# A two-layer hybrid decoder: inputs laid out as blocks, and the first stage's modulation wholly on TensorE in four column blocks beside ten feature tiles of w_in

## The chip, the core and the metric

The kernel runs on one core of a Trainium2 chip. The metric is the device time in microseconds of one execution, the median of several runs. Beside it stands one profiled execution, whose span, from its first to its last instruction, all rows of the trace are measured in. PE is TensorE (matmuls), DVE VectorE, ACT ScalarE, POOL GpSimd; SP issues most of the DMAs.

## What is computed

256 tokens of 2048 features go through two layers, each with a token-mixing block and a gated MLP of 5632 features, both behind a modulated RMS norm whose shift, scale and gate come from a conditioning vector c:

```python
cond = jax.nn.silu(c)
for l in range(DEPTH):
    mods = cond @ w_ada[l] + b_ada[l]
    sh1, sc1, g1, sh2, sc2, g2 = [m[:, None, :] for m in jnp.split(mods, 6, axis=-1)]
    h = rms_norm(x, norm_pre_mix[l]) * (1.0 + sc1) + sh1
    y = token_mixing(h, ...)           # proj = h @ w_in[l]; four head groups; concat @ w_out[l]
    x = x + g1 * rms_norm(y, norm_post_mix[l])
    h = rms_norm(x, norm_pre_ffn[l]) * (1.0 + sc2) + sh2
    y = conv_ffn(h, ffn_w_in[l], ffn_conv_w[l], ffn_w_out[l])
    x = x + g2 * rms_norm(y, norm_post_ffn[l])
```

w_ada is [2048, 12288] for each layer. The four head groups of token_mixing are a latent attention (MLA), a diagonal state-space model (S5), a sparse attention (NSA) and a gated delta rule (GDN, four heads, a chain of chunk products). All of it is f32.

## The kernel before

**Weights.** A weight tile is 128 x 1024 f32, 512 KB. wload issues its DMA on SP into one of four raw buffers; wsplit makes a high part wh on ACT (line 366) and a low part wl on DVE (line 367), three buffers each; mm3 multiplies the three products of the parts that matter on PE (line 127), 24 matmuls of 256 columns for a feature-major tile. mm3's other operand is the normed input ht, split the same way, or the other way round.

**Modulation.** w_ada passes as tiles of the same size. Most of it is background: ada streams blocks through two rawa buffers and sums 16 tiles on DVE (line 412), a given number of tiles with each weight tile. Only shift and scale of the first norm of layer 0 are needed at once. ada_quarter computes them in four quarters of the features, 16 tiles each, loaded at line 457 in two pieces of 2 KB a partition. Six tiles of a quarter (ADA_DVE) are summed on DVE into acc, ten go to PE as two matmuls with one stationary column, condc, into rows 0 and 32 of a PSUM bank, and acc follows with a column of ones. Quarters 1 to 3 take their tiles from the two rawa and the two rawm buffers in turn. A quarter ends in a copy, four transposes (lines 465 to 478) and the sums that make mod.

**The first stage (run).** x is loaded, its squares summed on ACT (new_squares), its row factors put on a diagonal (set_diag), and pre_norm multiplies x by that diagonal on PE, a quarter of the features at a time, with mod applied on ACT at line 549. Behind each quarter come the w_in tiles that need it: FIRST names three column groups of 256, so 12 tiles in all, the first four loaded ahead. Two of the three feed S5, the third the queries of GDN heads 0 and 1. Meanwhile DVE and ACT build the S5 tables. Some 25 small per-feature vectors are loaded by DMAs of their own and transposed on PE (vectors_ada, vectors); those of layer 1, and the loads of its S5 parameters b and c, stand in the FFN of layer 0.

**The mixers** of a layer follow in this order: S5, the narrow token-major columns (gemm_a), GDN heads 0 and 1 (gdn_half), heads 2 and 3, MLA, NSA, GDN's output gate, then project_out with w_out. The code says what depends on what; a scheduler lays the instructions of each engine in a fixed order, with the priorities that high_priority and the lanes give. So w_in products stand wherever a chain of small steps waits.

## Time and profile before

| what | us |
|---|---|
| median of 3 runs | 2695.22 |
| the three runs | 2687.34 to 2700.55 |
| span of the profiled execution | 2692.3 |
| PE busy in it | 2553.3 (95%) |
| DVE busy | 1924.8 (71%) |
| ACT busy | 1260.7 (47%) |
| end of the first stage (S5's first products) | 162.61 |
| first products of w_out, layer 0 | 527.37 |

For the profiled execution the record has the span; the median of the runs stands 2.9 us above it. The busy time of an engine is summed over its instructions without overlaps. The PE clock of a stretch is the mean of what was granted, 1.0 for 2.4 GHz and 0.5 for 1.2 GHz. The table of stretches gives the busy time of each engine and the mean share of the 16 DMA engines; the timeline joins instructions of one kind that follow each other, and a start is exact while a matmul's end is modelled.

### The profile page before, as it was taken

How to read it: one execution, taken by the hardware profiler on the slowest of the kernel's cores; microseconds unless marked ns; L12 is line 12 of the kernel's file. 1: busy time of each engine (PE TensorE's matmuls, PEld its weight loads, DVE VectorE, ACT ScalarE, POOL GpSimd, SP SyncE). 2: the span in 40 equal slices, each digit the busy share in tenths (PEclk: the TensorE clock that was granted, in tenths of full speed). 3: DMA queues.
4: the chain of work that ended last, by engine and by line, in shares of the span. 5: the costliest groups of instructions: out<-in, count | busy, mean ns of one | idle time of the engine just before them, and what ended most of it. 6: DMA issues, size and time to landing. Idle time of an engine off the chain costs nothing. (4 is left out here: it accounts for less than half of the span.)

```text
span 2692.3 us, 44696 instructions
## 1 busy us (share of the span) xinstructions
PE 2553.3 (95%) x17587; PEld 2257.8 (84%) x17587; DVE 1924.8 (71%) x3036; ACT 1260.7 (47%) x2025; POOL 9.6 (0%) x21
## 2 busy tenths in 40 slices
PE   5899999798999999999998999999899999999998
PEld 2478788687999999988877879888799999998886
DVE  6668888778877777776878888865677655555555
ACT  4244554546545444444545445555544444444443
POOL 0000000000000000000000000000000000000000
PEclk7889999899999999999999999999999999999999
DMA  8986887676888888877776667835588766665554
GB/s 269 298 242 188 259 277 226 202 268 217 274 287 277 283 286 284 293 247 234 232 255 228 189 201 243 267 123 170 180 272 280 224 187 188 183 186 188 188 188 148
DMA packets 325899, 621.43 MB, mean 231 GB/s; under 512 B 45132, under 2 KB 131640, under 8 KB 324152
## 3 DMA queue, kind: packets, MB, share of 16 engines
q1 hardware_dynamic: 317632, 617.36, 71.5%
q8 instruction: 138, 2.26, 0.3%
q10 hardware_dynamic: 8056, 1.21, 0.3%
q14 instruction: 73, 0.60, 0.1%
HBM read 614.26 MB, written 4.23 MB: 230 GB/s over the span
## 5 line engine op out<-in xcount | busy, mean ns | idle before, releaser
L127 PE MATMUL mm<-ht,wh 128*128 128x256 f32 x7232 | 1311.4, 283 | 2.9 <-ACT wh L366 2.9
L366 ACT CAST wh<-raw 128x1024 fp32r<-128x1024 f32 (+1 forms) x740 | 771.2, 1043 | 953.8 <-PE mm L127 751.2
L367 DVE TENSOR_TENSOR wl<-raw,wh 128x1024 fp32r<-128x1024 f32 (+1 forms) x740 | 893.2, 1213 | 346.1 <-ACT wh L366 344.2
L127 PEld LDWEIGHTS mm<-ht,wh 128*128 128x128 f32 x7232 | 1114.1, 189 | 15.2 <-issue 6.8
L127 PE MATMUL mm<-ht,wl 128*128 128x256 f32 x3616 | 1023.9, 283 | 7.9 <-DVE wl L367 7.6
L127 PEld LDWEIGHTS mm<-ht,wl 128*128 128x128 f32 x3616 | 681.7, 189 | 20.2 <-DVE wl L367 12.8
L412 DVE SCALAR_TENSOR_TENSOR acc<-rawa,condc,acc 128x1024 f32<-128x1024 f32 x310 | 397.3, 1282 | 216.5 <-DMA rawa<-in_w_ada_dram 215.0
L127 PE MATMUL mm<-wh,ht 128*128 128x512 f32 (+1 forms) x1600 | 507.4, 395 | 3.4 <-ACT ht L366 2.9
L127 PEld LDWEIGHTS mm<-wh,ht 128*128 128x128 f32 x1600 | 300.9, 189 | 68.0 <-ACT ht L366 3.2
L127 PE MATMUL mm<-wl,ht 128*128 128x512 f32 (+1 forms) x800 | 316.1, 395 | 1.7 <-DVE wl L367 1.7
L127 PE MATMUL mx<-wh,ht 128*128 128x512 f32 x704 | 221.4, 395 | 0.0
L127 PE MATMUL mx<-arena 128*128 128x128 f32 (+8 forms) x1432 | 199.1, 280 | 12.5 <-ACT arena L1417 4.7
L127 PEld LDWEIGHTS mx<-arena 128*128 128x128 f32 (+5 forms) x1432 | 156.0, 170 | 51.4 <-issue 20.2
L127 PEld LDWEIGHTS mm<-wl,ht 128*128 128x128 f32 x800 | 151.6, 190 | 34.0 <-DVE wl L367 3.0
L127 PEld LDWEIGHTS mx<-wh,ht 128*128 128x128 f32 x704 | 132.0, 187 | 32.1
L127 PE MATMUL mx<-wl,ht 128*128 128x512 f32 x352 | 139.3, 396 | 0.9 <-DVE wl L367 0.8
L131 PE MATMUL mx<-ident,arena 128*128 128x128 f32 (+3 forms) x367 | 68.4, 290 | 32.4 <-ACT arena L1280 11.0
L367 DVE TENSOR_TENSOR ht<-arena,ht 128x1024 fp32r<-128x1024 f32 x52 | 63.6, 1223 | 39.4 <-ACT ht L366 39.0
L131 PEld LDWEIGHTS mx<-ident,arena 128*128 128x128 f32 (+3 forms) x367 | 44.4, 148 | 53.7 <-ACT arena L1280 12.7
L1557 DVE SCALAR_TENSOR_TENSOR arena<-mm,v,arena 128x255 f32<-128x255 f32 (+1 forms) x176 | 78.2, 476 | 4.3 <-ACT arena L1555 3.5
L127 PEld LDWEIGHTS mx<-wl,ht 128*128 128x128 f32 x352 | 66.0, 187 | 18.1 <-DVE wl L367 2.1
L366 ACT CAST ht<-arena 128x1024 fp32r<-128x1024 f32 x52 | 54.2, 1050 | 56.5 <-PE mm L127 32.3
(308 smaller groups left out, 1514.1 us busy)
## 6 DMA issues: line engine op xcount, KB each, us to landing
raw<-in_ffn_w_in_dram SPq DMA_DIRECT2D x352, 512.0 KB
rawa<-in_w_ada_dram SPq DMA_DIRECT2D x348, 512.0 KB
raw<-in_ffn_w_out_dram SPq DMA_DIRECT2D x176, 512.0 KB
raw<-in_w_in_dram SPq DMA_DIRECT2D x116, 512.0 KB
raw<-in_w_out_dram SPq DMA_DIRECT2D x64, 512.0 KB
rawm<-in_w_ada_dram SPq DMA_DIRECT2D x28, 512.0 KB
raw<-in_w_in_dram SPq DMA_DIRECT2D x16, 426.0 KB
raw<-in_w_in_dram SPq DMA_DIRECT2D x16, 354.0 KB
```

The source lines that it names most:

```text
L127: self.nc.tensor.matmul(out, lhsT=lhsT, rhs=rhs, start=start, stop=stop)
L131: self.nc.tensor.transpose(out, in_, self.ident[:k, :k])
L366: self.nc.scalar.copy(hi.bitcast(F32R), src)
L367: self.nc.vector.tensor_sub(lo.bitcast(F32R), src, hi)
L412: self.last_mac = self.nc.vector.scalar_tensor_tensor(acc, w, self.condc[:, kc:kc + 1], acc, op0=ALU.mult, op1=ALU.add)
L1557: nc.vector.scalar_tensor_tensor(c[:, s:], ps[m][:, :256 - s], self.fconv(l, 2 - s, f), c[:, s:], op0=ALU.mult, op1=ALU.add)
```

## The change

A function layout on the host writes every weight matrix as a sequence of blocks (class Blocks), one for each tile in the form in which the kernel loads it, so that a tile is one DMA in which each partition's row is contiguous, 4 KB for most. The per-feature vectors become one array vec of 486 columns for each layer, loaded by two DMAs at the start; S5's b and c, the positions, the conditioning vector and a transposed x (xT) are laid out too. The kernel then takes its tiles from blk.

ada_quarter becomes a generator. All 16 tiles go to PE: the stationary operand condz holds a column of c and 31 zeros, and even and odd tiles go to different halves of the bank, so that the two matmuls of two tiles have four column blocks (o = 0, 32, 64, 96). The tiles take turns in two rawa, two rawm and two acc buffers. Four matmuls with ident2 sum the blocks into columns. row_scale takes the squares of xT on ACT, sums them on PE and scales xT on DVE; norm_quarter applies mod on DVE. With that new_squares of layer 0 moves into project_out.

FIRST has five column groups, so 20 w_in tiles of layer 0 stand in the first stage, interleaved with pairs of modulation tiles (the ten feature tiles of 128 columns are those five groups of 256); the keys and values of GDN heads 0 and 1 come with them and their convolutions are early. Layer 1 still takes three of the groups. The S5 tables are built between the tiles of quarters 2 and 3.

The core of the diff (the layout's calls in the rest of the kernel are all of the form of the one in gemms_b):

```diff
-FIRST = (O_U, O_U + 256, O_GQ)      # columns of the first products
...
+FIRST = (O_U, O_U + 256, O_GQ, O_GK, O_GV)
...
+    def blk(self, nm, l, k0, kn, *segs):
+        o, w = BLOCKS[nm].at[k0, kn, segs]
+        src = self.I[nm]
+        return bass.AP(tensor=src.tensor, offset=src.offset + l * BLOCKS[nm].n + o, ap=[[w, P], [1, w]])
...
-    def ada_quarter(self, q, rings, on_dve):
-        """Shift and scale of a quarter of the features for the first block, without delay; on_dve: the chunks whose products
-        go to the vector engine, the others to the tensor engine."""
+    def ada_quarter(self, q):
         nc = self.nc
         bank = self.mx()
-        rows = [bank[32 * i:32 * i + 1] for i in range(2)]
-        src = self.I["w_ada"][0][:, 0:2 * D].rearrange("k (i c) -> k i c", i=2)[:, :, q * 512:(q + 1) * 512]
-        acc = self.acct()
-        for c in range(4):
-            self.mm(bank[0:64, c * P:(c + 1) * P], self.zerob[:, 0:64], self.identb, c == 0, c == 3)
-        def add(col, t, first, last):
+        for kc in range(KT):
+            pool, nm = ((self.rawa, "rawa"), (self.rawm, "rawm"), (self.accp, "acc"))[kc % 3]
+            w = pool.tile([P, 1024], F32, name=nm, tag=nm)
+            nc.sync.dma_start(w, self.blk("w_ada", 0, kc, 1, (q * 512, 512), (D + q * 512, 512)))
             for i in range(2):
-                self.mm(rows[i], col, t[:, i * 512:(i + 1) * 512], first, last)
-        pe = [kc for kc in range(KT) if kc not in on_dve]
-        for kc in range(KT):
-            pool, nm = ((self.raw, "raw"), (self.rawa, "rawa"), (self.rawm, "rawm"))[rings[kc % len(rings)]]
-            w = pool.tile([P, 1024], F32, name=nm, tag=nm)
-            nc.sync.dma_start(w.rearrange("p (i c) -> p i c", i=2), src[kc * P:(kc + 1) * P])
-            if kc in on_dve:
-                self.ada_mac(acc, w, kc, kc == on_dve[0])
-            else:
-                add(self.condc[:, kc:kc + 1], w, kc == pe[0], False)
-        add(self.ones[:, 0:1], acc, False, True)
+                o = 64 * (kc % 2) + 32 * i
+                self.mm(bank[o:o + 32], self.condz[:, kc], w[:, i * 512:(i + 1) * 512], kc < 2, kc >= KT - 2)
+            if kc % 2 and kc < KT - 1:
+                yield
         with self.first():
-            r = self.reg(AT[7], 512)(512)[0:64]
-            nc.scalar.copy(r[:, 0:256], bank[0:64, 0:256])
-            nc.vector.tensor_copy(r[:, 256:512], bank[0:64, 256:512])
+            r = self.small.tile([P, 512], F32, name="hf", tag="hf")
+            nc.scalar.copy(r[:, 0:256], bank[:, 0:256])
+            nc.vector.tensor_copy(r[:, 256:512], bank[:, 256:512])
+            cols = self.mx(8)
             for c in range(4):
-                self.tp(bank[:, c * 64:(c + 1) * 64], r[:, c * P:(c + 1) * P])
-            cols = bank[:, 0:256].rearrange("p (c i z) -> p i c z", i=2, z=32)
+                self.mm(cols[:, 2 * c:2 * c + 2], r[:, c * P:(c + 1) * P], self.ident2[:, 0:64:32], True, True)
+            cols = cols.rearrange("p (c i) -> p i c", i=2)
             for i in range(2):
-                self.ada_out(0, 2 * i + q // 2, cols[:, i, :, 0], 4 * (q % 2))
+                self.ada_out(0, 2 * i + q // 2, cols[:, i], 4 * (q % 2))
...
+    def row_scale(self):
+        nc = self.nc
+        xT = self.ar[:, A_X:A_X + 4096]
+        for i in range(4):
+            nc.sync.dma_start(xT[:, i * 1024:(i + 1) * 1024], self.I["xT"][:, i * 1024:(i + 1) * 1024])
+        r = self.reg(AT[7], 2048)
+        sq, (v, y, a) = (r(512), r(512)), (r(256) for _ in range(3))
+        ss = self.mx(256)
+        for i in range(8):
+            nc.scalar.activation(sq[i % 2], xT[:, i * 512:(i + 1) * 512], AF.Square)
+            for j in range(2):
+                self.mm(ss, self.ones, sq[i % 2][:, j * 256:(j + 1) * 256], i + j == 0, i + j == 8)
+        nc.vector.tensor_scalar(v, ss, 1.0 / D, EPS, op0=ALU.mult, op1=ALU.add)
+        self.rsqrt(v, y, a)
+        for i in range(4):
+            t = xT[:, i * 1024:(i + 1) * 1024].rearrange("p (k t) -> p k t", k=4)
+            nc.vector.tensor_tensor(t, t, y[:, None, :].to_broadcast([P, 4, 256]), op=ALU.mult)
+        self.xr = xT
+    def norm_quarter(self, q):
+        nc = self.nc
+        for k2 in (2 * q, 2 * q + 1):
+            h = self.small.tile([P, 512], F32, name="hf", tag="hf")
+            o = k2 % 2 * 512
+            hi, lo = (self.ht[4 * i + k2 // 2][:, o:o + 512] for i in range(2))
+            for i in range(2):
+                k = 2 * k2 + i
+                sh, sc = (self.mod[:, 0, 2 * j + k // 8, k % 8:k % 8 + 1] for j in range(2))
+                nc.vector.tensor_scalar(h[:, i * 256:(i + 1) * 256], self.xr[:, k * 256:(k + 1) * 256], sc, sh,
+                                        op0=ALU.mult, op1=ALU.add)
+            self.split(h, hi, lo)
...
-    def gemms_b(self, W, cols, nm, kc, pre=()):
-        """Several of them, as a generator that stops after every kc chunks of the contraction; pre: weight tiles loaded
-        ahead."""
+    def gemms_b(self, l, cols, nm, kc, tiles=False):
         kn = 1024 // (nm * P)
-        banks = [self.mmt() for _ in cols]
-        parts = [[b[:, m * 256:(m + 1) * 256] for m in range(nm)] for b in banks]
-        pre = list(pre)
+        parts = [[b[:, m * 256:(m + 1) * 256] for m in range(nm)] for _, b in cols]
         for kk in range(0, KT, kc):
-            for c0, ps in zip(cols, parts):
+            for (c0, _), ps in zip(cols, parts):
                 for k0 in range(kk, kk + kc, kn):
-                    w = self.wsplit(pre.pop(0)) if pre else self.wtile(1024, self.parts_b(W, c0, nm, k0))
+                    w = self.wtile(self.blk("w_in", l, k0, kn, (c0, nm * P)))
                     for ki in range(kn):
                         k = k0 + ki
                         for m in range(nm):
                             o = (ki * nm + m) * P
                             self.mm3(ps[m], [i[:, o:o + P] for i in w], self.hk(k), k == 0 and m == 0,
                                      k == KT - 1 and m == nm - 1)
-            yield
+                    if tiles:
+                        yield
+            if not tiles:
+                yield
...
-    def first_gemms(self, l, pre=()):
-        return self.gemms_b(self.I["w_in"][l], FIRST, 2, KT // 4, pre)
+    def first_gemms(self, l):
+        if l:
+            return self.gemms_b(l, [(c, self.mmt()) for c in FIRST[:3]], 2, KT // 4)
+        self.lane = 0
+        return self.gemms_b(l, [(c, self.mmt() if i < 4 else self.mx()) for i, c in enumerate(FIRST)], 2, KT // 4, True)
...
+        early = [conv(0, i, ps) for i, ps in enumerate(first_qkv)] if l == 0 else []
...
         for tt in range(2):
             self.nc.sync.dma_start(self.x[:, tt], src[tt * P:(tt + 1) * P])
+        if l == 0:
+            self.new_squares()
...
             if not last and g == 0:
                 self.new_squares()
-                rg = self.reg(A_SCR, 800)
-                self.vectors_ada(l + 1, rg)
-                self.vectors(l + 1, rg)
...
         next(constants)
-        self.condition()
         next(constants)
-        rg = self.reg(A_GA + 2560 + P + KT, 800)
-        self.vectors_ada(0, rg)
+        self.vectors()
+        self.lane = 1
+        a = self.ada_quarter(0)
+        next(a)
         self.finish(constants)
+        self.lane = 0
+        self.row_scale()
         self.lane = 1
-        self.ada_quarter(0, (0, 1, 0, 2), ADA_DVE)
-        for tt in range(2):
-            nc.sync.dma_start(self.x[:, tt], xin[tt * P:(tt + 1) * P])
-        self.xx = self.const.tile([P, 8], F32, name="xx")
-        self.new_squares()
-        self.set_diag(self.x_stats())
-        h = self.pre_norm(0, 0)
-        next(h)
-        self.lane = 0
-        self.vectors(0, rg)
-        pre = [self.wload(self.parts_b(self.I["w_in"][0], c0, 2, 0)) for c0 in FIRST[:4]]
-        g = self.first_gemms(0, pre)
-        macs = [self.last_mac]
+        self.finish(a)
+        self.norm_quarter(0)
+        tables = itertools.chain(self.s5_tables(0, nc.scalar, self.ar[:, AT[6]:AT[6] + 1024]),
+                                 self.s5_rotations(0, (self.ar[:, AT[4]:AT[4] + 1024], self.ar[:, AT[5]:AT[5] + 1024])))
+        g = self.first_gemms(0)
         for q in range(1, 4):
             self.lane = 1
-            self.ada_quarter(q, (1, 2), ADA_DVE)
-            macs.append(self.last_mac)
-            self.lane = 0
-            next(g)
-            self.lane = 1
-            if q < 3:
-                next(h)
+            a = self.ada_quarter(q)
+            n = len(FIRST)
+            for i in range(n):
+                next(g)
+                for _ in range(8 * (i + 1) // n - 8 * i // n):
+                    next(a, None)
+                if q > 1:
+                    self.lane = 0
+                    next(tables, None)
+                    next(tables, None)
+                    self.lane = 1
+            self.norm_quarter(q)
         self.lane = 0
-        self.finish(self.s5_tables(0, nc.scalar, self.ar[:, AT[6]:AT[6] + 1024]))
-        with self.after(macs[1]):
-            self.finish(self.s5_rotations(0, (self.ar[:, AT[4]:AT[4] + 1024], self.ar[:, AT[5]:AT[5] + 1024])))
```

**SP at the end of the first stage.** The rows are DMAs in the order of the queue; rawa, rawm and acc hold w_ada, raw holds w_in. Before:

```order
L457 DMA rawa_758<-in_w_ada_dram 128x2x512
L457 DMA rawm_762<-in_w_ada_dram 128x2x512
L349 DMA raw_807<-in_w_in_dram 128x4x256
L349 DMA raw_837<-in_w_in_dram 128x4x256
L349 DMA raw_1154<-in_w_in_dram 128x4x256
L349 DMA raw_1184<-in_w_in_dram 128x4x256
L349 DMA raw_1218<-in_w_in_dram 128x4x256
L349 DMA raw_1535<-in_w_in_dram 128x2x426
```

and after the change:

```order
L406 DMA raw_1157<-in_w_in_dram 128x1024
L406 DMA raw_1250<-in_w_in_dram 128x1024
L406 DMA raw_1280<-in_w_in_dram 128x1024
L406 DMA raw_1314<-in_w_in_dram 128x1024
L406 DMA raw_1344<-in_w_in_dram 128x1024
L406 DMA raw_1377<-in_w_in_dram 128x1024
L406 DMA raw_1736<-in_w_in_dram 128x852
L406 DMA raw_1757<-in_w_in_dram 128x852
L499 DMA rawa_1187<-in_w_ada_dram 128x1024
L499 DMA rawm_1191<-in_w_ada_dram 128x1024
L499 DMA acc_1195<-in_w_ada_dram 128x1024
L499 DMA rawa_1199<-in_w_ada_dram 128x1024
```

The last w_ada tile stood ahead of the w_in tiles; now the last four stand behind eight raw loads.

**PE inside a quarter.** mx1 is the bank of the modulation, the second name of a pair is the stationary column, or the normed input for mm. Before, in the first quarter:

```order
L127 MATMUL mx1_161<-rawa_170,condc_107 1x512 x2
L127 MATMUL mx1_161<-rawm_177,condc_107 1x512 x2
L127 MATMUL mx1_161<-rawa_184,condc_107 1x512 x2
L127 MATMUL mx1_161<-rawm_191,condc_107 1x512 x2
L127 MATMUL mx1_161<-raw_195,condc_107 1x512 x2
```

and after the change, in the second quarter:

```order
L228 MATMUL mx1_323<-acc_362,arena_58 32x512
L228 MATMUL mx1_323<-rawa_366,arena_58 32x512 x2
L228 MATMUL mx1_323<-rawm_370,arena_58 32x512 x2
L228 MATMUL mx1_323<-acc_374,arena_58 32x512 x2
L228 MATMUL mm_290<-ht_59,wh_380 128x256 x2
L228 MATMUL mx1_323<-rawa_408,arena_58 32x512 x2
L228 MATMUL mm_290<-ht_59,wl_381 128x256
```

The products now have 32 columns of output and every ring feeds them; the w_in tiles stand between.

**PE in the chain of GDN heads 2 and 3.** mx with arena alone is a product of the chain, mx with ident a transpose, mm a w_in product, rawm a weight of MLA. Before:

```order
L127 MATMUL mx_3279<-arena 128x128 x4
L127 MATMUL mm<-ht,wl 128x256
L127 MATMUL mm<-ht,wh 128x256 x2
L127 MATMUL mm<-ht,wl 128x256
L127 MATMUL mm<-ht,wh 128x256 x2
L127 MATMUL mm<-ht,wl 128x256
L127 MATMUL mm<-ht,wh 128x256
L127 MATMUL mx_3285<-arena 128x128 x4
L127 MATMUL mm<-ht,wh 128x256
L127 MATMUL mm<-ht,wl 128x256
```

and after the change:

```order
L228 MATMUL mx_3183<-arena 128x128 x4
L228 MATMUL mx_3745<-arena,rawm 128x256 x2
L232 MATMUL mx_3189<-ident,arena 128x128 x4
L228 MATMUL mx_3745<-arena,rawm 128x256 x2
L228 MATMUL mx_3195<-arena 128x128 x4
L228 MATMUL mx_3755<-rawm,arena 128x256 x3
L228 MATMUL mx_3205<-arena 128x128 x4
L228 MATMUL mx_3765<-rawm,arena 128x256 x2
L232 MATMUL mx_3211<-ident,arena 128x128 x4
L228 MATMUL mx_3765<-rawm,arena 128x256
```

The w_in products between the chain's steps are gone, and MLA's products stand there.

## Rows read from the trace of the kernel before

**Rows 1.** The page: busy time, share of the span and instructions of each engine
```profile
PE 2553.3 (95%) x17587; PEld 2257.8 (84%) x17587; DVE 1924.8 (71%) x3036; ACT 1260.7 (47%) x2025; POOL 9.6 (0%) x21
```

**Rows 2.** Stretches of the start: busy us and count by engine, PEclk, DMA share, GB/s
```profile
0.00:10.00 10.00, 1.51 (x7) 0.94 (x7) 4.27 (x18) 0.00 (x0) 3.52 (x10) 1.00 0.70 217
...
35.00:40.00 5.00, 4.09 (x18) 0.58 (x14) 4.72 (x19) 3.81 (x11) 0.00 (x0) 0.93 1.02 415
...
58.00:146.00 88.00, 74.17 (x409) 35.68 (x408) 48.41 (x87) 19.64 (x38) 0.14 (x2) 0.87 0.91 299
```

**Rows 3.** Waits of PE in 0:160 and of SP's queue in 60:150: total, times, longest
```profile
PE mx L127 <- DMA rawa<-in_w_ada_dram: 6.2, 4, 3.1
...
SPq L457 <- PE mx L127: 36.9, 25, 3.9
```

**Rows 4.** PE's timeline, first stage and mixers: start, length, what, count, idle before
```profile
66.63 1.03 PE L127 MATMUL mx<-rawm,condc 128*1 128x512 f32 x4
...
67.58 0.39 PE L127 MATMUL mm<-ht,wl 128*128 128x256 f32 x1
...
83.97 1.03 PE L127 MATMUL mx<-acc,ones 128*1 128x512 f32 x4
...
88.88 0.60 PE L127 MATMUL mx<-rawm,condc 128*1 128x512 f32 x2
...
162.61 0.48 PE L127 MATMUL mx<-arena 64*128 64x128 f32 x2
...
326.79 0.28 PE L127 MATMUL mm<-ht,wl 128*128 128x256 f32 x1
...
332.11 0.28 PE L127 MATMUL mm<-ht,wl 128*128 128x256 f32 x1
```

**Rows 5.** Stretches of the mixers, all work, then the weight products (mm) alone
```profile
162.60:334.70 172.10, 165.14 (x1053) 138.53 (x1053) 146.85 (x296) 81.29 (x156) 0.00 (x0) 0.98 0.75 218
...
334.70:399.40 64.70, 62.48 (x488) 55.47 (x486) 53.73 (x81) 33.22 (x64) 0.52 (x1) 1.00 0.89 278
...
415.20:461.90 46.70, 45.73 (x413) 41.33 (x412) 39.11 (x72) 21.95 (x47) 0.00 (x0) 1.00 0.71 222
...
415.20:461.90 46.70, 26.95 (x157) 20.49 (x156) 1.66 (x4) 1.55 (x4) 1.00 0.71 222
```

**Rows 6.** PE's timeline: first GDN decay, chain products, first products of w_out
```profile
334.69 0.39 PE L127 MATMUL mx<-tri,gg 128*128 128x128 f32 x2
...
461.01 1.08 PE L127 MATMUL mx<-arena 128*128 128x128 f32 x8
...
461.93 0.28 PE L127 MATMUL mx<-ident,ry 128*128 128x128 f32 x1
...
527.37 0.80 PE L127 MATMUL mm<-wh,ht 128*128 128x512 f32 x1 [2.90 <-ACT ht L366]
```

**Rows 7.** DVE's timeline inside the chain of GDN heads 2 and 3
```profile
446.62 1.23 DVE L367 TENSOR_TENSOR wl<-raw,wh 128x1024 fp32r<-128x1024 f32 x1 [0.62 <-ACT wh L366]
...
447.76 0.68 DVE L1030 TENSOR_TENSOR arena<-mx,lmask 128x512 f32<-128x512 f32 x1
```

**Rows 8.** Waits of PE in 770:900 (FFN of layer 0) and 160:480 (mixers)
```profile
PE mx L131 <- DMA rawm<-in_s_c_re_dram: 3.9, 1, 3.9
...
PE mx L131 <- ACT rawm L1280: 1.3, 3, 0.5
...
PE mx L127 <- DMA rawm<-in_nsa_w_v_dram: 2.1, 2, 1.8
...
PE mx L127 <- DMA rawm<-in_mla_w_ukv_dram: 1.2, 1, 1.2
```

**Rows 9.** A stretch of the softmax tail
```profile
505.50:511.00 5.50, 5.50 (x21) 4.20 (x22) 2.73 (x5) 2.88 (x11) 0.00 (x0) 0.58 0.62 179
```

**Rows 10.** ACT's timeline: a square of x, and the last split ahead of w_out
```profile
42.73 0.63 ACT L575 ACTIVATE junk<-arena 128x512 bf16<-128x512 f32 x1
...
526.27 1.04 ACT L366 CAST ht<-arena 128x1024 fp32r<-128x1024 f32 x1 [2.05 <-DVE arena L709]
```

More of the change, by code (lines that the diff above doesn't have):

```diff
@@ L799, in mla @@
                       self.rsin[:, tt, 0:32], 4, 32)
-        wk = part("mla_w_ukv", 2, 0, 4, 256, 0, P)
+        wk = part("mla_w_ukv", 2, range(4), 256, 0, P)
         for hp in range(2):
@@ L807, in mla @@
             nc.scalar.copy(kn[:, 2 * hp:2 * hp + 2], ps.rearrange("p (h t) -> p h t", h=2))
-        wk = part("mla_w_ukv", 2, 0, 4, 256, P, P)
+        wk = part("mla_w_ukv", 2, range(4), 256, P, P)
         for tt in range(2):
@@ L1182, in s5_tables @@
         t = lambda: r(16)
-        are, aim, ls = (self.sld[:, l, i * 16:(i + 1) * 16] for i in range(3))
+        are, aim, ls = (self.vs(l, "s5")[:, i * 16:(i + 1) * 16] for i in range(3))
         step, mag, th, sn, cs, tmp = (t() for _ in range(6))
```

346 lines of the change are left out of this document (171 added, 175 removed).

## The prediction

> **What bounds the kernel now.** The page's first part comes first: TensorE (PE) is busy for 2553.3 us, 95% of the span [rows 1]. A change therefore pays where it takes work off PE, or where it shortens one of the few stretches in which PE is held up. The table by stretches finds the first such stretch at the start. In 58 to 146 us PE has 74.17 busy us of 88 at a mean granted clock of 0.87, while the DMA engines have a share of 0.91 and move 299 GB/s [rows 2]. Two things hold the transfers there. The queue waits of SP show 36.9 us on PE's modulation products: four w_ada buffers are all there is, and PE has to free them. PE in turn waits for w_ada tiles [rows 3]. The PE timeline then gives the milestones [rows 4]: the first stage ends when S5 begins, at 162.61 us, and by then 12 w_in tiles have been multiplied.
>
> The table of the mixers says that from there on PE is the bound for a while: 165.14 busy of 172.10 us before the decay of the first two GDN heads, 62.48 of 64.70 behind it, and 45.73 of 46.70 us during the decay-to-output chain of heads 2 and 3 [rows 5, 6]. Of those 46.70 us, 26.95 hold weight products, which fill the gaps of the chain [rows 5]. Only then comes the attention tail up to the output projection at 527.37 us [rows 6].
>
> **Part 1: eight w_in tiles leave the mixers.** FIRST grows from 3 to 5 column groups, 12 to 20 tiles. In the mixers' pure stretch 45 weight matmuls start between 326.79 and 332.11 us [rows 4], 0.118 us each, so a tile of 24 costs 2.84 us and eight cost 22.7 us. PE is the bound where they stood, so they come off the span there: **-22.7 us**, if the first stage takes them in for nothing.
>
> **Part 2: the end of the first stage.** The order of SP gives what has to come before the last w_ada tile: 64 w_ada tiles, 20 w_in tiles of 0.524 MB, two of 0.436 MB and 2.1 MB of xT, together 47.1 MB. The first 10 us move at a mean of 217 GB/s [rows 2], so about 4 us are lost at the start. The rate is the unknown. From below it is the 299 GB/s of the old stage; from above the 415 GB/s of the five us in which the long rows of x land [rows 2]. The old stage at a full share would be 299/0.91 = 329. I take 355, between the two, as every tile now is one contiguous block and six w_ada buffers stand where four did: 133 us. Behind the last tile come its landing and product, 2 us, the chain from the last product to the next features, 4.9 us (83.97 to 88.88 in the old quarters [rows 4]), and the five w_in tiles that need it, 5 x 2.84 = 14.2 us. In all 4 + 133 + 2 + 4.9 + 14.2 = 158 us against 162.6: **-5 us**. The bounds are 182 (+20) at 299 GB/s and 143 (-20) at 415, rounded.
>
> PE has to keep up with that. Four modulation products of 512 columns take 0.95 us from their start to the next matmul at 66.63 [rows 4], where eight of 128 columns, a quarter of a product each, take 0.92 us [rows 6]: at that rate four in a row would be 1.84 us, so two column groups run side by side. Of such a tile a quarter has 16, so 15 us at two groups and half that at four; five w_in tiles add 14. That is 22 to 29 us of PE for 21 tiles, which need 31 us of transfer at 355 GB/s: close, but covered. DVE loses its six tiles a quarter, which nobody waited for long. The Trainium skill says, in "TensorEngine Tiling (Array Packing)", Tiling Modes, that different tiles of the array can execute in parallel; the trace agrees for two, with the 0.95 us above, and shows none with four. By that rule it is the 22.
>
> One detail is against it. The last four w_ada tiles stand on SP behind eight raw loads, and with four raw and three wh buffers the last of those eight can be issued only when 15 w_in tiles are done on PE. I get that point at about 130 us, in step with the transfers, so I charge nothing; late PE would push it into the end of the stage.
>
> **Part 3: what the mixers lose as cover.** Those tiles were filling. In the new order the chain of GDN heads 2 and 3 has no weight product in it, only about 68 matmul passes of 256 columns of MLA, 8 us at 0.118 us. PE's own work in the old chain is 45.73 - 26.95 = 18.8 us [rows 5]. If the chain keeps its 46.7 us, PE idles for 46.7 - 18.8 - 8 = 20 us; if the weight products were what stretched it, not at all. One look inside decides: at 447.76 DVE begins an eviction that had been standing behind a wl split of 1.23 us that started at 446.62 [rows 7]. About 7.4 tiles stood there by the order of PE, so some 9 us of the chain was such waiting: exposed 11 us, **+11**, with 0 to +20 as bounds.
>
> **Part 4: small loads.** In the FFN of layer 0 PE waits 3.9 us for s5_c_re and 1.3 for the copies behind it, and in the mixers 2.1 us for nsa_w_v and 1.2 us for mla_w_ukv [rows 8]. C of S5 is now one contiguous load without transposes, the layer-1 vectors are two loads at the start, the mixers' tiles are contiguous: up to **-9** with what a clock drop behind the waits costs; at worst 0. I take -8. The row scaling on DVE and ACT, the constants' new place and the S5 tables lie beside the w_ada stream and cost nothing as long as that stream ends the stage; Weights of the rest of the kernel only change layout; PE is the bound there, so nothing.
>
> new_squares of layer 0 now stands in project_out: eight squares of 0.63 us on ACT, seven of them ahead of the last split of the mixers' outputs. ACT was idle for 2.05 us before that split, waiting for DVE, and PE waits 2.90 us for it [rows 6, 10]. So 0 to +4 us; **+1**, because the wait for DVE's norm covers most.
>
> **Sum:** -22.7 - 5 + 11 - 8 + 1 = -23.7 on the profiled span of 2692.3, so 2668.6 us. The median shown, 2695.22, is 2.9 above that span: 2671.5, rounded **2671 us**.
>
> **Rivals.**
> (A) The layout does not do what it says: the queue moves no more than 299 GB/s, or PE frees its buffers no faster. Then the first stage ends at 182 us and -5 becomes +20: 2696 us, no change. For it: the page's DMA share was already 0.91 [rows 2], with pieces of 2 KB. Against: 36.9 us of queue waits on PE at four buffers [rows 3]. The Trainium skill, "DMA: Bandwidth & Descriptors", Specifications, asks for at least 512 B for full rate, and 1 and 2 KB pieces are above that; by that rule the longer rows would bring nothing and the time would be A's. The 415 GB/s of the 8 KB rows of x speak for some gain.
> (B) The mixers are a chain, not PE's work: from the first decay (334.69) to the output projection (527.37) stay 192.7 us [rows 6]. In the new order weight products of 4.3 tiles more, 12 us, stand between the first stage and that decay, so it comes at 158 + 172.1 + 12 = 342 and the projection at 535, 7.5 us later than now. With -8 + 1 behind it and 2.9 to the median: 2696 us, no change.
> (C) Four column blocks at once and 415 GB/s: the stage ends at 143. Then -20 instead of -5: 2656 us.
> (D) The slower side: the uncovered chain drops PE's clock. Around the softmax tail, where PE idles, the granted clock reads 0.58 [rows 9], near the lower level of 1.2 GHz. If heads 2 and 3 run so, their 18.8 us of PE work take twice as long and nothing of B's chain shrinks: 2696 + 18.8 = 2715 us. It decides from the point where the uncovered chain takes longer than the old 46.7 us. Against it: MLA's products and half the evictions are still there, and the chain loses DVE's wl splits.
>
> **How the numbers follow.** Forecast 0.50 (2656 to 2687 by its own bounds on rate and cover), A 0.13, B 0.12, C 0.15, D 0.10. The predicted time is the forecast's, 2671. The range goes from 2646 to 2704: it holds A, B and C's centre and leaves out D and the far half of C's spread. A measurement of this kernel tells 0.5%, 13.5 us, from no change, so faster means under 2681.7. Faster: C and nine tenths of the forecast's half, and a little of A and B, 0.65; same: most of A and B and a little of the forecast, 0.24; slower: D and the tails, 0.11.
>
> **What would show it.** Right: S5's first products at 150 to 165 us with 20 tiles done, over 330 GB/s from 20 to 130 us, modulation products four to a start; the projection at about 505 to 515 us; PE waits of some 10 us inside the second GDN chain; no wait for s5_c. Wrong: a first stage that ends beyond 175 us (A, and the SP row where the last four w_ada tiles wait says whether the raw loads did it); a projection at or after 527 us with idle PE (B), with a granted clock near 0.5 to 0.6 in the second chain (D). A gain outside layer 0's first 530 us and its FFN's S5 loads would be one that I do not see.

## The result and the profile after

The changed kernel takes 2716.6 us (2708.3 to 2720.9) where the kernel before took 2694.0 (2687.3 to 2700.6) on the same chip: 1.0093 times as long, 95% interval 1.0069 to 1.0116. It is slower by 22.6 us; 2671 was predicted, with a range that ended at 2704. The profiled execution of after has a span of 2706.5 us, 14.2 more than before's.

The page's first part, and three rows of the stretches of the first stage (columns as in [rows 2]):

```profile
PE 2579.7 (95%) x17604; PEld 2283.8 (84%) x17604; DVE 1909.8 (71%) x3018; ACT 1258.6 (47%) x2001; POOL 10.2 (0%) x22
...
43.00:73.60 30.60, 25.72 (x147) 14.97 (x146) 22.35 (x41) 5.89 (x8) 0.28 (x2) 0.88 0.70 262
73.60:128.80 55.20, 48.00 (x321) 27.98 (x321) 14.94 (x36) 20.20 (x48) 0.00 (x0) 0.97 0.60 225
...
155.80:174.30 18.50, 7.28 (x27) 1.76 (x26) 4.12 (x11) 2.07 (x4) 0.00 (x0) 0.70 0.88 323
```

Only the first 43 us move more than before (345 GB/s against 289). From there to 128.8 us the queue stays under before's 299 GB/s [rows 2]: the DMA share falls to 0.60 while PE is busy for 48.00 of 55.20 us. The waits of SP's queue and of PE in 0:192 say who held whom (total, times, longest):

```profile
SPq L499 <- PE mx L228: 90.5, 21, 10.9
...
PE mx L228 <- DMA rawa<-in_w_ada_dram: 8.7, 3, 8.2
```

SP waits 90.5 us for PE to free w_ada buffers; of these 61.4 lie in 60 to 150 us, where before it waited 36.9 [rows 3]. PE's timeline shows why, and the milestones (start, length, what, count, idle before):

```profile
23.00 0.60 PE L228 MATMUL mx<-rawm,arena 128*32 128x512 f32 x2
23.02 0.60 PE L228 MATMUL mx<-acc,arena 128*32 128x512 f32 x2
23.43 0.60 PE L228 MATMUL mx<-rawm,arena 128*32 128x512 f32 x2
...
110.18 1.05 PE L228 MATMUL mx<-acc,arena 128*32 128x512 f32 x2
111.16 0.39 PE L228 MATMUL mm<-ht,wl 128*128 128x256 f32 x1
...
164.18 1.92 PE L228 MATMUL mx<-rawa,arena 128*32 128x512 f32 x4 [8.16 <-DMA rawa<-in_w_ada_dram]
...
191.48 1.24 PE L228 MATMUL mx<-arena 64*128 64x128 f32 x8
...
369.04 0.39 PE L228 MATMUL mx<-tri,gg 128*128 128x128 f32 x2
...
530.20 0.50 PE L228 MATMUL mm<-wh,ht 128*128 128x512 f32 x1 [1.59 <-ACT ht L423]
...
581.84 1.22 PE L228 MATMUL mx<-ident,ry 128*128 128x128 f32 x4 [5.14 <-DVE ry L256]
```

An f32 product leaves two records, and the two products of a w_ada tile four. At 23 us four column blocks do run at once: four records start together every 0.43 us. Where one product stands alone between weight products (110.18), its two records follow each other and hold PE for 0.98 us, as much as the four records of a whole tile before [rows 4]. The third quarter takes 42.1 us (83.7 to 125.8), not 31, and PE is busy for most of it:

```profile
83.70:125.80 42.10, 36.84 (x242) 21.39 (x241) 11.39 (x27) 18.28 (x45) 0.00 (x0) 1.00 0.66 250
```

The modulation products hold PE for 15.5 of these 36.84 us, the weight products for 16.2, transposes and table products for 5; PE's waits are 5.1 us, all for ACT and none for a DMA. The last four w_ada tiles, behind eight raw loads on SP, cost an 8.16 us wait. So S5 starts at 191.48, not at 162.61 [rows 4], the first GDN decay at 369.04, not at 334.69 [rows 6].

That decay is 34.4 us late. Not quite half of it comes back behind the decay: NSA's last spread (the row at 581.84) stood at 563.22 before, 18.6 us earlier. PE is less busy there. Stretches of the later mixers of after, the last of them with the weight products (mm) alone; then one of before:

```profile
400.00:600.00 200.00, 169.70 (x1087) 142.61 (x1087) 153.04 (x372) 100.43 (x234) 3.23 (x3) 0.91 0.66 224
...
580.00:590.00 10.00, 5.29 (x29) 4.10 (x30) 8.74 (x22) 6.62 (x17) 0.00 (x0) 0.51 0.65 213
...
442.00:491.00 49.00, 0.00 (x0) 0.00 (x0) 1.57 (x4) 1.51 (x4) 0.93 0.54 190
```

```profile
400.00:600.00 200.00, 181.29 (x1176) 152.65 (x1175) 152.24 (x314) 99.17 (x219) 2.27 (x2) 0.97 0.72 231
```

Behind the mixers the casts of weight tiles on ACT serve as a measure: there are 740, and the n-th stands for the same work in both kernels. The 121st, 301st, 421st and last of after, then of before:

```profile
698.28 1.05 ACT L423 CAST wh<-raw 128x1024 fp32r<-128x1024 f32 x1 [1.12 <-PE mm L228]
...
1228.84 1.05 ACT L423 CAST wh<-raw 128x1024 fp32r<-128x1024 f32 x1
...
1646.43 1.05 ACT L423 CAST wh<-raw 128x1024 fp32r<-128x1024 f32 x1 [1.87 <-PE mm L228]
...
2685.84 1.05 ACT L423 CAST wh<-raw 128x1024 fp32r<-128x1024 f32 x1 [1.76 <-PE mx L228]
```

```profile
678.94 1.05 ACT L366 CAST wh<-raw 128x1024 fp32r<-128x1024 f32 x1 [0.41 <-PE mm L127]
...
1222.47 1.04 ACT L366 CAST wh<-raw 128x1024 fp32r<-128x1024 f32 x1
...
1641.44 1.05 ACT L366 CAST wh<-raw 128x1024 fp32r<-128x1024 f32 x1 [1.11 <-PE mm L127]
...
2671.86 1.05 ACT L366 CAST wh<-raw 128x1024 fp32r<-128x1024 f32 x1 [1.75 <-PE mx L127]
```

After is late by 19.3, 6.4, 5.0 and 14.0 us. Three things happened: the mixers end 18.6 us late; the FFN of layer 0 gives back 12.9 (its wait for s5_c_re [rows 8] is gone); and from the 421st cast on 9.0 us are lost, where nothing was thought to change. There the groups of one product, by shape, in 1900:2600 (count, busy us, mean ns of one), read for after and before:

```profile
L228 PE MATMUL mm<-ht,wh 128*128 128x256 f32 x2816 | 507.5, 282 | 0.0
```

```profile
L127 PE MATMUL mm<-ht,wh 128*128 128x256 f32 x2816 | 500.5, 281 | 0.0
```

The same products start 120.0 ns apart instead of 118.3. One difference was in sight: all raw, wh and wl tiles lie 128 bytes further on in each partition, because the vectors take other room. wh began at byte 170112 of the partition, which is 128 beyond a multiple of 256, and now begins on a multiple of 256.

### The profile page after: what moved, and what is told of

It reads as the page before. It is cut to its first block, busy times and chain, and to the rows that moved or that the text cites. A ratio compares the mean times of both kernels' runs of the same rounds, so it can differ in the third digit from the quotient of the medians.

```text
span 2706.5 us, 44498 instructions
## 1 busy us (share of the span) xinstructions
PE 2579.7 (95%) x17604; PEld 2283.8 (84%) x17604; DVE 1909.8 (71%) x3018; ACT 1258.6 (47%) x2001; POOL 10.2 (0%) x22
## 3 DMA queue, kind: packets, MB, share of 16 engines
q10 hardware_dynamic: 1008, 1.06, 0.1%
## 5 line engine op out<-in xcount | busy, mean ns | idle before, releaser
L462 DVE SCALAR_TENSOR_TENSOR acc<-rawa,condc,acc 128x1024 f32<-128x1024 f32 x300 | 384.5, 1282 | 148.1 <-DMA rawa<-in_w_ada_dram 146.7
L424 DVE TENSOR_TENSOR ht<-arena,ht 128x1024 fp32r<-128x1024 f32 x52 | 63.6, 1223 | 39.9 <-ACT ht L423 39.6
L1607 DVE SCALAR_TENSOR_TENSOR arena<-mm,vec,arena 128x255 f32<-128x255 f32 (+1 forms) x176 | 78.3, 476 | 6.2 <-ACT arena L1605 5.3
L228 PE MATMUL mx<-rawm,arena 128*18 128x256 f32 (+3 forms) x248 | 74.5, 494 | 2.1 <-DMA rawm<-in_w_ada_dram 1.3
L232 PE MATMUL mx<-ident,arena 128*128 128x128 f32 (+1 forms) x328 | 59.7, 286 | 11.5 <-ACT arena L807 5.6
```

The lines of the kernel that those rows point to most:

```text
L228: self.nc.tensor.matmul(out, lhsT=lhsT, rhs=rhs, start=start, stop=stop)
L232: self.nc.tensor.transpose(out, in_, self.ident[:k, :k])
L424: self.nc.vector.tensor_sub(lo.bitcast(F32R), src, hi)
L462: self.nc.vector.scalar_tensor_tensor(acc, w, self.condc[:, kc:kc + 1], acc, op0=ALU.mult, op1=ALU.add)
L1607: nc.vector.scalar_tensor_tensor(c[:, s:], ps[m][:, :256 - s], self.fconv(l, 2 - s, f), c[:, s:], op0=ALU.mult, op1=ALU.add)
```

## Experiments

The theory had three parts: the longer first stage; the order of PE, with too much weight work ahead of the first decay and none left between the later chains; and the 128 bytes. Ratios are to the kernel before, measured beside each experiment, with 95% intervals. In the diffs `...` stands for what is left out.

**The queue: e1_ahead.** The last four w_ada transfers go ahead of the raw loads.

```diff
-            nc.sync.dma_start(w, ...)
+            with self.first() if q == 3 and kc >= 12 else ExitStack():
+                nc.sync.dma_start(w, ...)
...
```

> The changed kernel with one edit: the DMAs of the last four w_ada tiles get a high priority, so that they stand ahead of the eight raw loads on SP and not behind them. Theory 1 (the end of the first stage waits for that queue): PE's 8.2 us wait for rawa at 155.8 us disappears, the half clock behind it too, S5 begins at about 176 us and not at 190, and the time falls by 10 to 16 us from 2716.6. Rival (the transfers would come that late anyway, or the mixers take the time back): at most 3 us.

2713.0, ratio 1.0062 (1.0045 to 1.0078). The last w_ada product comes at 162.7 instead of 169.2, S5 at 184.7 (176 was expected), the first decay at 366.9, NSA's end at 580.3. The queue is worth between 2 us (the traces, at the mixers' end) and 8 us (the ratios, whose intervals overlap), less than the 10 to 16 expected.

**The tiles: e2_first3.** The new modulation and layout, but three column groups (12 tiles) in the first stage, as before.

```diff
-        ... [(c, self.mmt() if i < 4 else self.mx()) for i, c in enumerate(FIRST)] ...
+        ... [(c, self.mmt()) for c in FIRST[:3]] ...
...
-            n = len(FIRST)
+            n = 3
```

> The changed kernel with three column groups in layer 0's first stage as before, 12 w_in tiles instead of 20; the other eight go back to the mixers. Theory 1 (the first stage has no room for them): S5 begins at about 160 to 168 us, the mixers take 22.7 us more PE work but cover the chain of GDN heads 2 and 3 again; the time is 5 to 15 us below 2716.6. Rival B (the chain from the GDN decay on sets the end, whatever stands between): the decay comes at about 345 us and w_out's last group follows it at the same distance, so 20 us or more below. If the move were a gain as forecast: 15 to 20 us above 2716.6.

2684.8, ratio 0.9961 (0.9946 to 0.9976). The second and third quarters take 32 and 30 us, the last one 39; S5 starts at 160.48, the decay at 336.8, NSA ends at 559.5. So the eight extra tiles cost 32 us, which is rival B's 20 or more and not theory 1's 5 to 15; without them the change is a gain.

**The layout: e3_oldrows.** The weights stay matrices, read in pieces of 1 and 2 KB.

```diff
-    out = {nm: b.lay(a[nm]) for nm, b in BLOCKS.items()}
+    out = {nm: a[nm] for nm in BLOCKS}
...
```

> The changed kernel with the big weights (w_ada, w_in, w_out, the FFN's, MLA's) left as the matrices they were, so that tiles are loaded in pieces of 1 and 2 KB again; all else is the changed kernel. If the blocks speed the transfers: the first 45 us move 10% less, the first stage ends 3 to 10 us later, 2720 to 2727. If they do nothing: 2716 and the same trace. A third theory: rows of 4 KB slow the weight products (their pitch in the FFN of layer 1 is 120.0 ns, it was 118.3): then the pitch is 118.3 again and the time some 10 us lower.

2713.7, ratio 1.0068 (1.0048 to 1.0089), within the uncertainty of after's. Nothing measurable hangs on the long rows here: in the first 43 us, where the DMA engines are fullest (a share of 0.94 and 0.89), e3 moves 346 GB/s and after 345. The Trainium skill, "DMA: Bandwidth & Descriptors", Specifications, puts the least transfer for line rate at 512 B, which the old pieces of 1 and 2 KB exceed; the trace agrees, with these two rates. That was what the prediction weighed as rival A's ground.

**The 128 bytes: e4_pad, e5_first3_pad, e7_before_shift, e11_before_256.** One unused tile ahead of raw. e4 puts 128 bytes into after, e5 into e2_first3, e7 into the kernel before; e11 puts 256 into the kernel before (64 for 32 in the edit).

```diff
+        self.pad = self.const.tile([P, 32], F32, name="pad")
         self.raw = pool("raw", 4)
```

> The changed kernel with 128 bytes a partition left free ahead of the raw buffers, which moves raw, wh, wl, rawa, rawm, acc and what follows by 128 bytes, to the places modulo 256 that they had before. If the pitch of the weight products hangs on that place: 118.3 ns in the FFN of layer 1 instead of 120.0, and 10 to 18 us less over the kernel. If it is a property of the execution or of the instruction stream: 2716.6 within 0.3%, pitch 120 or whatever this execution has.

> The changed kernel with three column groups in the first stage and the 128 bytes of padding, the edits of the second and the fourth experiment together. If the two causes are independent: 2684.8 - 16 = 2669 us (2664 to 2674), pitch 118.3 ns. If the padding's gain came from something in the order of the five-group kernel: 2680 to 2685.

> The kernel before with 128 bytes a partition of padding ahead of the raw buffers, which puts wh and wl where the changed kernel has them (a multiple of 256 bytes). If the place sets the pitch: 120.0 ns in the FFN of layer 1 instead of 118.3, and 2693.8 + 12 to 18 = 2706 to 2712 us. If the changed kernel's pitch had another cause: 2693.8 within 0.2%.

> The kernel before with 256 unused bytes per partition put ahead of the raw tiles (e7_before_shift put 128 there): all of raw, wh and wl lie 256 bytes further on, so that their place modulo 256 is that of the kernel before again (128). If the pitch of the products goes by the place modulo 256: 118.33 ns in the feed-forward part of layer 1, as before, and 2694 us within 0.3%. Rival (any shift, or the larger space taken, or the copy of the program, makes the difference): 120.0 ns as in e7_before_shift, and 2697 to 2711.

The same group of products as above, in e4, e7 and e11:

```profile
L229 PE MATMUL mm<-ht,wh 128*128 128x256 f32 x2816 | 500.5, 281 | 0.0
```

```profile
L128 PE MATMUL mm<-ht,wh 128*128 128x256 f32 x2816 | 507.5, 282 | 0.0
```

```profile
L128 PE MATMUL mm<-ht,wh 128*128 128x256 f32 x2816 | 500.5, 281 | 0.0
```

The pitch goes with the place modulo 256 in every trace: 118.3 ns at 128, 120.0 at 0, whichever kernel it is; a shift by 256 changes nothing. What it is worth in the medians is less sure, and the expectations for the time held in e4 and e11 alone. e4 is at 2700.8, ratio 1.0023 (1.0004 to 1.0041), 16 us under after; e5 at 2681.3, 0.9932 (0.9908 to 0.9957), 0.3% under e2, where its rival had it and not at 2669; e7 at 2700.2, 1.0013 (0.9993 to 1.0032), no measurable loss against before, where 2706 to 2712 was expected; e11 at 2695.2, 0.9991 (0.9977 to 1.0006). The traces agree better: from the 421st cast to the last, 1030.4 us pass in before and 1040.7 in e7, 1039.4 in after and 1029.3 in e4, so 10 us each time. Ahead of the 421st cast the pitch differs as well (118.3 and 120.0 ns in 700:1250), but other differences cover it there.

**The columns: e6_pairs, e12_first3_fours.** With the 128 bytes and e1's step, the four products of two w_ada tiles are issued right behind one another; e12 does the same with three groups.

```diff
...
+            pair = pair + [(kc, w)] if kc % 2 else [(kc, w)]
+            if kc % 2:
+                for i in range(2):
+                    for k, t in pair[::-1]:
+                        o = 64 * (k % 2) + 32 * i
+                        with self.first():
+                            self.mm(bank[o:o + 32], self.condz[:, k], t[...], ...)
...
```

> The changed kernel with the padding (2700.8), the last four w_ada DMAs ahead of the raw loads, and the modulation matmuls of two tiles issued as four in a row, the later tile's first and with a high priority, so that no w_in tile stands between them. Theory 1a (PE takes about 1 us a tile where halves stand alone, 14.5 us a quarter instead of 7): quarters of 33 us instead of 41, S5 at about 162 us, the time 20 us lower, 2680. Rival (transfers set the quarter: buffers and latency of the queue): quarters stay at 38 to 41 us, 2695 to 2700. Rival B (the mixers' chain takes all that is given to it back): S5 earlier, the decay not.

> e5_first3_pad with the two steps of e6_pairs: the four column blocks of two chunks are issued one right behind the other, and the last four transfers of w_ada go ahead of the raw loads. If the columns of the modulation bound the first stage here too, its last column comes at about 140 instead of 151, and the time is 2671 to 2676. Rival (in e5_first3_pad the first stage is bound by the bytes of w_ada and of ten tiles of w_in, and the quarter that comes earlier only moves weight products of the mixers ahead of the decay): the decay within 5 us of 341, time 2678 to 2684.

e6: 2689.3, 0.9966 (0.9946 to 0.9986). The third quarter takes 37 us and the last 33, where e4 needs 42 and 44, so the products that stood alone were part of the cost. S5 starts at 176.2, 11.7 us earlier than in e4 (187.9; e1's step alone gave 6.8), though not at the expected 162. The decay, at 360.0, is only 4.8 earlier than e4's 364.8, but NSA's end, at 567.3, again 10.7. e12: 2677.8, 0.9927 (0.9901 to 0.9953), against 0.9932 without: the same.

**DVE ahead of the decay: e8_rate0.** After with the 128 bytes; no background w_ada tile is summed in the first part of the mixers.

```diff
-        bg = ((((0, (4, 5, 8, 6, 9, 7)),), (0.5, 0.6, 1, 0.8)), ...
+        bg = ((((0, (4, 5, 8, 6, 9, 7)),), (0.0, 0.6, 1, 0.8)), ...
```

> The changed kernel with the padding (2700.8) and no background modulation tile with the weight tiles of layer 0's first mixers (rate 0 instead of 0.5 up to the first GDN decay), which takes about 28 sums of 1.28 us off DVE between S5 and the decay and puts them later. Theory 2 (that stretch is DVE's and S5's chain, PE only fills it with tiles it could take later): the stretch shrinks from 178 to about 150 us, the end of layer 0's mixers comes 15 to 25 us earlier, 2680 to 2690. Rival (PE's work bounds the stretch, as forecast): it stays within 5 us of 178 and the time at 2700 or above, as the sums have to be made up later.

2749.7, ratio 1.0194 (1.0155 to 1.0232). The decay stays where it was (364.9). S5 started at 193.8, 6 us later than in e4, so the stretch between is 171 us, far from theory 2's 150: DVE is not what holds it. Behind the decay these sums do cost time: NSA's end comes at 552.4, 25.6 us earlier than in e4. But they only moved behind it, where nothing covers them, as PE's wait in 540:720 shows:

```profile
PE mx L229 <- DVE acc L484: 71.1, 2, 38.0
```

**The order: e9 to e18.** BOOST says by how many steps of its schedule the scheduler puts the weight stream ahead of the mixers' arithmetic. With 300 for 2500 fewer weight products stand ahead of the first decay on PE: 46.7 tiles instead of 60.0 in after, 39.9 instead of 47.7 in before. The first stage keeps 4000. In e9 (on e6), e10 (on e5), e13 (on after), e15 (on before):

```diff
-BOOST = 2500
+BOOST = 300
...
-        return self.tc.high_priority(BOOST + 1500)
+        return self.tc.high_priority(4000)
```

e14 (on e5), e16 (on after), e17 (on before) and e18 (on e12) go back to 2500 behind layer 0's mixers:

```diff
             self.project_out(l, self.mixers(l, g))
+            self.boost = 2500
             self.drain()
```

> e6_pairs with one number changed: the weight stream of w_in is put 300 instead of 2500 steps ahead of the mixers' arithmetic (the first stage keeps its own lead of 4000). On PE's order the first GDN decay then stands behind 46.7 tiles of weight products instead of 62.0. Theory A (what stands ahead of the decay costs its full price there, and only about half of it comes back behind): the decay comes 15.3 tiles x 2.84 us = 43 us earlier, at 317 instead of 360.0; behind it the mixers take longer, and their end (the last spread of NSA, 567.3 in e6_pairs) comes 19 to 24 us earlier, at 543 to 548; time 2665 to 2670. Rival B (all the mixers' products together are the bound: what leaves the stretch ahead of the decay comes back behind it whole): the decay at 317 to 330, but the end within 5 us of 567, time 2684 to 2692. Rival C (the weight stream starves, since casts are asked for later): casts fall behind, products of weights are missing before the feed-forward part, 2700 or more.

> e5_first3_pad with the weight stream of w_in put 300 instead of 2500 steps ahead of the mixers' arithmetic: the first GDN decay stands behind 40.5 tiles instead of 51.8. Theory A: the decay 11.3 x 2.84 = 32 us earlier, at about 309 instead of 341.5, the end of the mixers 14 to 18 us earlier than 564.2, time 2663 to 2668. Rival B: the end within 5 us of 564, time 2676 to 2685. Rival C: 2690 or more.

> The changed kernel with one number changed and nothing else: the weight stream stands 300 instead of 2500 steps ahead of the mixers' arithmetic (the first stage keeps its lead of 4000). The first GDN decay then stands behind 46.7 tiles of weight products instead of 60.0. Theory A (products used up ahead of the decay are missing as filling between the chains of 400 to 600): the decay comes 13.3 tiles x 1.6 to 2.8 us = 21 to 37 us earlier than 369.0, and TensorE is busy over 190 of the 200 us of 400 to 600 instead of 169.7; the mixers' end comes 15 to 25 us earlier than 581.8; time 2690 to 2702, if what e9_fours_boost300 lost after its mixers (its 16.0 us wait at 600 to 660, 11 us in layer 1) is lost here in part. Rival B (the order is not the cause): the end within 5 us of 581.8, 2710 to 2720.

> The kernel before with the same one number changed (300 instead of 2500): the first GDN decay stands behind 39.9 tiles instead of 47.7. By theory A the kernel before gains too, with no other edit: the decay 7.8 tiles x 1.6 to 3.3 us = 12 to 26 us earlier than 334.7, the mixers' end 8 to 20 us earlier than 563.2, time 2676 to 2689. Rival B (only the changed kernels' order has something to give): the end within 5 us of 563, 2690 to 2698.

> e10_first3_boost300 with the lead of 300 in layer 0's mixers alone; from the sums between the parts on it is 2500 again. The casts of e10_first3_boost300 fell back against e5_first3_pad's from 22.6 us ahead to 16.2 ahead between the 300th and the 480th, in layer 1's mixers. If the lead makes that: 6 us less than 2669.3, so 2663, and the casts stay 22 us ahead. Rival (layer 1's mixers lose it for another reason): 2669 within 3.

> The changed kernel with the lead of 300 in layer 0's mixers alone (e13_after_boost300 without its layer 1). The casts of e13_after_boost300 ran 12.7 us ahead of the changed kernel's at the 112th to 120th, when the feed-forward part of layer 0 begins, and fell 19 us back between the 380th and the 480th, in layer 1's mixers. If the lead makes the second part too: about 12 us less than the changed kernel's 2716.6, so 2698 to 2708. Rival (what is gained in layer 0's mixers is lost behind them anyway): 2711 to 2720.

> The kernel before with the lead of 300 in layer 0's mixers alone. In e15_before_boost300 the casts were 2.4 us ahead of the kernel before at the 112th, 5 at the 300th, and fell back by 9 to 23 us in layer 1's mixers. If the lead makes that: 2 to 10 us less than 2694, so 2684 to 2692; then most of what e14_first3_boost300_l0 gained (46 us) is no matter of the lead alone, but of the change with three feature tiles in the first stage. Rival (the lead alone makes the gain of e14_first3_boost300_l0): 2650 to 2665.

> e14_first3_boost300_l0 with the two steps of e6_pairs (the four column blocks of two chunks right behind one another, the last four transfers of w_ada ahead). e12_first3_fours against e5_first3_pad gained 3.5 us by these: 2641 to 2648. Rival (it only moves PE's work about, as in e9_fours_boost300, which lost again behind the mixers what it gained in them): 2649 to 2662.

Measured (decay: first `mx<-tri,gg`; end: NSA's last spread; BOOST is 300 throughout or in layer 0's mixers, l0):

| kernel | first stage | BOOST | S5 | decay | end | us | ratio (interval) |
|---|---|---|---|---|---|---|---|
| before | 12 tiles, old | 2500 | 162.6 | 334.7 | 563.2 | 2694.0 | 1 |
| e15 | 12 tiles, old | 300 | 166.4 | 323.7 | 558.8 | 2702.2 | 1.0021 (1.0006 to 1.0037) |
| e17 | 12 tiles, old | 300 l0 | 166.7 | 321.4 | 556.9 | 2689.1 | 0.9986 (0.9969 to 1.0002) |
| after | 20 tiles | 2500 | 191.5 | 369.0 | 581.8 | 2716.6 | 1.0093 (1.0069 to 1.0116) |
| e13 | 20 tiles | 300 | 188.2 | 346.4 | 555.4 | 2711.5 | 1.0063 (1.0041 to 1.0085) |
| e16 | 20 tiles | 300 l0 | 184.5 | 342.9 | 554.2 | 2698.5 | 1.0007 (0.9992 to 1.0022) |
| e9 | 20 tiles, fours, 128 B | 300 | 173.7 | 335.2 | 544.8 | 2688.9 | 0.9973 (0.9953 to 0.9993) |
| e5 | 12 tiles, 128 B | 2500 | 164.7 | 341.5 | 564.2 | 2681.3 | 0.9932 (0.9908 to 0.9957) |
| e10 | 12 tiles, 128 B | 300 | 152.5 | 304.0 | 538.3 | 2669.3 | 0.9890 (0.9858 to 0.9922) |
| e14 | 12 tiles, 128 B | 300 l0 | 152.6 | 298.0 | 528.1 | 2648.7 | 0.9826 (0.9804 to 0.9848) |
| e18 | 12 tiles, fours, 128 B | 300 l0 | 152.7 | 300.5 | 527.0 | 2643.9 | 0.9822 (0.9798 to 0.9847) |

In after the one number brings the mixers' end 26.4 us forward (e13), more than their lateness of 18.6. PE in 400:600, in e13 and then e14, whose first row is the decay:

```profile
400.00:600.00 200.00, 196.62 (x1255) 165.32 (x1255) 165.23 (x361) 114.01 (x246) 3.23 (x3) 0.99 0.74 254
```

```profile
298.01 0.38 PE L229 MATMUL mx<-tri,gg 128*128 128x128 f32 x2
...
400.00:600.00 200.00, 188.61 (x1173) 158.22 (x1171) 168.32 (x372) 109.90 (x229) 3.23 (x3) 0.98 0.77 260
```

PE is busy 196.62 us in e13, 169.70 in after: the products kept back fill the gaps. But e13 loses it again, twice. PE's one wait at the end of the mixers, ahead of the norm of the FFN, grows: in 600:660, after, then e16:

```profile
PE mx L228 <- issue: 9.5, 1, 9.5
```

```profile
PE mx L228 <- issue: 15.0, 1, 15.0
```

And the mixers of layer 1 are slower with 300: the 361st cast of e13 is 5.5 us ahead of after's, the 421st 17.0 behind. e16 leaves layer 1 alone and keeps its lead there (9.1 ahead at the 421st), 2698.5, as expected. Other expectations failed. e9's decay came 25 us earlier, not 43; its mixers' end came where theory A had it (544.8), its total where rival B had it, at e6's. e13's total likewise is rival B's, 2711.5 and not 2690 to 2702. e10 missed its 2663 to 2668 by 1 us. e15 gained 4.4 us at the mixers' end, not 8 to 20, and lost it in layer 1. e14 came 14 us under its expectation: its casts run 6 to 10 us ahead of e10's already from the 41st to the 105th, where both have the same order on PE (the granted clock in 160:400 is 1.00 in e14, 0.96 in e10), 6 more come in the FFN of layer 0, which has its old lead again, and 8 in layer 1. Why the first part differs is open. Nor is the order of the mixers all that the short lead changes: in e10 and e14 S5 starts 12 us earlier than in e5, and PE's 5.2 us wait for a w_ada tile in e5 is not there (the granted clock in 138:150 is 0.57 in e5, 0.72 in e10, 0.86 in e14). That is a third of the 37.5 us by which e10's decay comes earlier.

The change and the order depend on each other: the short lead is worth 0.14% to the kernel before (e17, not told from nothing), 0.86% to after (e16) and 1.06% to the new modulation with 12 tiles (e14 against e5). e17 and e18 came as expected. e18 takes 1.8% less than the kernel before and 2.7% of it less than after; its fours add nothing measurable to e14. With the short lead throughout, too, 12 tiles (e10) are 0.8% faster than 20 (e9, which has the fours besides).

## Why the prediction was wrong

- **What bounds the kernel**: right as to PE, wrong as to the conclusion. PE is the bound ahead of the first decay, but behind it, in 400 to 600, it had 18.7 idle us already before. Work taken off there does not come off the span in full.
- **Part 1, -22.7 if the first stage takes the tiles in for nothing**: that condition failed. The eight tiles came off the mixers, and cost more than that in the first stage: S5 started 28.9 us later, and with 12 tiles (e2) 2.1 earlier. e2 puts it at 32 us. This is the largest step that failed.
- **Part 2, 158 us**: it came at 191.48. The rate of 355 GB/s was taken as the bound; PE was, with 225 GB/s at a share of 0.60. The working of PE's side, 22 to 29 us a quarter, counted modulation and weight products only and took PE as filled without a gap. In the third quarter PE was busy for 36.84 of 42.10 us: the modulation products, often alone, took 15.5 and the weight products 16.2, near the upper bound, but 5 us of transposes and table products and 5 us of waits came on top. The upper bound of the rate was mis-added too: its terms at 415 GB/s give 139 us, not 143. The queue of the last four tiles, noted and charged with nothing, held S5 up by 6.8 us and the whole by 2 to 8 (e1). Rival A named the right place, PE freeing its buffers no faster, and was 9.5 us short.
- **Part 3, +11 for the second GDN chain**: the chain has no weight product, as predicted (442:491, `mm` 0.00), but PE was busy for 44.0 of those 49 us with MLA's and other work, so 5 us were exposed and not 11. The chain did not grow: from its decay (444.92) to DVE's last sum of it (489.24) 44.3 us pass, where before took 46.8. The loss sat later, in the attention chains and at NSA's end, where PE waited 5.14 us for a spread and the granted clock was 0.51 in 580:590, the lower level. D's mechanism, the clock, showed there; in the chain of heads 2 and 3 the granted clock was 0.93. That D's 2715 us is next to the measured time is luck.
- **Part 4, -8**: right in its direction. The wait for s5_c_re is gone, and the FFN of layer 0 gave back 12.9 us by the casts, more than the bound of 9; no run separates what the loads gave there. Nor does one separate the +1 for the squares of x: PE waits 1.59 us for the last split, where it waited 2.90 [rows 6].
- **Rival B** was the nearest in kind: the first decay later, and only part of it back. It put the decay at 342 and the projection 7.5 us late; the decay came at 369.0 and w_out's first products at 530.2, 2.8 us late. What it lacked was the late first stage and the end of NSA.
- **A term that was missing**: "Weights of the rest of the kernel only change layout; PE is the bound there, so nothing." The new constants shift wh by 128 bytes, and 7168 + 3584 products of 256 columns go from 118.3 to 120.0 ns. The traces show the pitch every time, and 10 us for it behind the 421st cast; the medians put the whole between no measurable loss (e7) and 16 us (e4 against after).

The sum as it was in the profile: +18.6 at the mixers' end, +0.7 to the 121st cast, -12.9, -1.4 and +9.0 to the end are +14.0; the medians say +22.6, as after's profile is of the shortest of its four executions. Where the other 8.6 us lie no trace shows.

## To carry to other kernels

Work that fills the gaps of later chains is not free to move: before a stage takes in more of it, look whether PE is already the bound there (a transfer queue that waits for PE says so, and 36.9 us of such waits stood in the rows of before [rows 3]), and what will fill the chains it leaves. A scheduler's lead is tuned for one balance: when a change moves work across a stage, try the lead again, for each part of the program by itself. And compare the pitch of an untouched inner loop before and after; it showed here what no line of the diff did.

## Unexpected in the hardware

- The records of four 32-column products of 512 columns, on four column blocks, start together every 0.43 us (23.00 to 23.43). The two records of a product that stands alone take 0.98 us (110.18), and the four of two products on two column blocks 0.99 (116.18 to 117.17). So here the full gain came only where four products stood together in PE's order. The Trainium skill, "TensorEngine Tiling (Array Packing)", Tiling Modes, says that different tiles of the array can run in parallel; the trace agrees for four.
- Products with wh and wl as the stationary operand stood 118.3 ns apart with the tiles' place at 128 modulo 256 bytes, 120.0 ns at 0, in all 20 traces (120.0 in after, e1, e2, e3, e7, e13 and e16, 118.3 in before and the others). Why, and which of the tiles that moved counts, is not known.
